# An encoder's second feed-forward layer: the sums of weights of all four units made in DRAM by accumulating transfers

## The chip, the core and the metric

One core of a Trainium2 chip runs the whole program. The metric is the device time of one execution in microseconds, of which the kernel before has three: 2171.28 (median), 2171.19 and 2171.61.

The core has five instruction streams: PE (TensorE, with its weight loads shown apart as PEld), DVE (VectorE), ACT (ScalarE), POOL (GpSimd) and SP (SyncE). Here SP does nothing but issue transfers, POOL issues the accumulating ones.

## The reference

Two layers over 256 positions of width 2048, in float32. Layer 0 has a mixer of pooling and attention, layer 1 one of matrix memory (mLSTM); each is followed by a gated MLP with a convolution of width 3 over positions. Cut to what matters here:

```python
def conv_ffn(x, w_up, conv_w, conv_b, w_down):
    u = x @ w_up
    up = jnp.pad(u, ((0, 0), (1, 1), (0, 0)))
    c = conv_w.astype(u.dtype)
    u = c[0] * up[:, :-2] + c[1] * up[:, 1:-1] + c[2] * up[:, 2:] + conv_b.astype(u.dtype)
    gate, val = jnp.split(u, 2, axis=-1)
    return (jax.nn.silu(gate) * val) @ w_down

def reference(...):
    for layer in range(DEPTH):
        ...
        x = x + mixed
        x = x + conv_ffn(rms_norm(x, norm_ffn[layer]), w_up[layer], conv_w[layer], conv_b[layer], w_down[layer])
    return x
```

`w_up` has 2048 x 11264 weights in each layer, `w_down` 5632 x 2048.

## The kernel before

**The stream of weights.** All weights pass through the class `Stream` in one order, in entries of up to 128 x 1024 values (512 KB). For each entry SP issues the load into a raw buffer `w`; ScalarE casts it to the high part of `hl` (line 164) and VectorE subtracts that from the raw values to get the low part (line 165). Three matmuls (high by high, high by low, low by high) then stand for one float32 matmul; all of them are recorded at line 285. Within a feed-forward layer up to 7 entries are loaded ahead and 3 split ahead; there are 7 raw buffers and 5 split ones, and a load waits until its raw buffer is free.

**The units.** An up-projection of one feature block is sixteen k-tiles (`up`, tile name `up`). Half of the blocks in the chunks 2 to 5 of a layer go another way, four blocks at a time: `quads` multiplies two by two blocks with seven products in place of eight (a Winograd form), on sums of activations (`sx`) and sums of weights; its tile is `p`. Such four blocks are a *unit*. A layer has four, in the chunks 2, 3, 4 and 5; the text calls them units 2, 3, 4 and 5 by their chunk. A unit takes 24 entries in a first part (16, called A and B below, in 8 pairs, and later 8 more, C) and four entries of plain weights (`b`). Between a unit's steps lie those of plain up-projections and of the down-projection (`dn`) of the chunk before.

**The table UNITS** has, for each unit, its chunk, its half, the first and last *slot* over which its steps are spread (a slot is one quarter of an `up` or two k-tiles of a `dn`, about one stream entry of plain weights), and a flag that says how its sums of weights come about:

- Flag 0: the raw weights are loaded as pieces of `in_q`, and VectorE makes the sums in the raw buffers, in `sums` (lines 144, 147, 149 and 150 of the profile): one add of 128 x 512 for an A entry, two for a B entry (the first of them reads the A entry's buffer too), one for a C entry. That is 32 adds a unit.
- Flag 1: the sums are made in DRAM ahead of time, in a tile `G` for each of the unit's eight pairs, and loaded like weights (kind "made" in `load`; an entry A or C is then two loads of 128 x 512, one from `G` and one from `in_q`).

**Making a pair in DRAM** is `make_step`, in four parts. Parts 0 and 1 each copy one half of the pair's rows from `in_q` to `G` on SP's queue (line 118), and then add other columns of `in_q` onto the copy by an accumulating transfer on POOL's queue (line 119). Parts 2 and 3 are accumulating transfers from `G` to `G` (line 123). The copies and the adds keep the program's order on their queues, so POOL waits at line 119 until the copy has landed. The list `places` says with which stream entry a pair's first part is issued and by how many entries the next ones follow.

Apart from PE, whose order is the program's, and the pinned instructions, a scheduler sets the order on each engine.

Of the kernel before, what the change touches and what calls it, by code (L numbers as in the profile page):

```python
# [64 lines left out]
class Stream:  # L65
# [56 lines left out]
            of = 0 if part == 2 else 1024  # L122
            pin(add.dma_start(G[:, at : at + 512], G[:, of : of + 512], accum_op=ALU.add))  # L123

    def prepare(self, kind, w):

        if kind[1] == 0:
            self.first = w
            return
        x, G = self.first, self.made_tile(kind[2])  # L130
        pin, add = self.tc.keep_in_program_order, self.nc.vector.tensor_add
        b11, b12, b22, b21 = (e[:, c : c + 512] for e in (x, w) for c in (0, 512))
        for to, other in ((b11, b12), (b12, b22), (b22, b11), (b21, b22)):
            pin(add(to, to, other))
        self.nc.gpsimd.dma_start(G[:, 0:1024], x)
        self.nc.gpsimd.dma_start(G[:, 1024:2048], w)

    def sums(self, i):
        if i in self.w and not self.w[i][4] and self.w[i][3] in ("sum", "chain", "left"):
            w, kind = self.w[i][0], self.w[i][3]  # L140
            l, r = w[:, 0:512], w[:, 512:1024]
            pin, add = self.tc.keep_in_program_order, self.nc.vector.tensor_add
            if kind == "sum":
                pin(add(r, r, l))
                self.sum = r
            if kind == "left":
                pin(add(l, l, r))
            if kind == "chain":
                pin(add(l, l, self.sum))
                pin(add(r, r, l))  # L150
            self.w[i][4] = True

    def split(self, then=None):
        i = self.n_split
        self.sums(i)
        w, n, width, kind = self.w.pop(i)[:4]
        if isinstance(kind, tuple):
            self.prepare(kind, w)
            self.n_split += 1
            self.sums(i + 1)  # L160
            return
        hl = self.home(i, False).tile([P, 2, CH * P], F32R, tag="hl", name=f"hl{i}")
        for c in range(0, width, n):
            (self.nc.vector.tensor_copy if i + c == 0 else self.nc.scalar.copy)(hl[:, 0, c : c + n], w[:, c : c + n])  # L164
            self.nc.vector.tensor_sub(hl[:, 1, c : c + n], w[:, c : c + n], hl[:, 0, c : c + n].bitcast(F32))  # L165
            then and then(c // n)
        self.hl[i] = hl
        self.n_split += 1
        self.sums(i + 1)

    def ahead(self, i, split=None):
        n = len(self.srcs)
        while self.n_load < min(n, i + self.la + 1):
            if self.n_load >= self.n_split + self.la - self.sa + 1:
                self.split()
            self.load()
        while self.n_split < min(n, i + (self.sa if split is None else split) + 1):
            self.split()

    def next(self):  # L180
        while self.is_prep(self.at):
            self.at += 1
        i = self.at
        self.ahead(i)
        self.at += 1
        return self.hl.pop(i)

    def is_prep(self, i):
        return isinstance(self.srcs[i], tuple) and isinstance(self.srcs[i][0], tuple)


class Weave:
# [6 lines left out]
    def add(self, gen, delay=0.0):  # L199
        self.q.append([self.t + delay, gen])  # L200
# [9 lines left out]
    def _run(self, e):  # L210

        try:
            d = next(e[1])
        except StopIteration:
            self.q.remove(e)
            return True
        e[0] = self.t + (d or 0.0)
        return d is not None
# [19 lines left out]
def trunk(ctx: ExitStack, tc: tile.TileContext, gx, xT, xn, call, catt, cml, weights, make, out):  # L238
# [239 lines left out]
    def attention_layer(norm, nxt):  # L478
        with ExitStack() as es:
# [11 lines left out]
            def block(ps, ti, dst, name):  # L491
# [33 lines left out]
                if name == "k":  # L525
                    yield from wv.wait(lambda: norm.blocks == NB)
                    fin = norm.finish()
                    yield next(fin)
                    rq = scales()
                    yield 4.0  # L530
                    for t in range(2):
                        r4 = rot[:, t, :].rearrange("p (h d) -> p h d", h=4)
                        v.tensor_mul(r4, r4, rq[:, 4 * t : 4 * t + 4].unsqueeze(2).to_broadcast([P, 4, P]))
                    yield 3.0
# [420 lines left out]
    def ffn_layer(layer, norm, nxt):  # L955
        with ExitStack() as es:
# [212 lines left out]
            for step in _ffn_plan(layer):  # L1169
                kind, c = step[:2]  # L1170
                key = step[:3]
                if key not in run:
                    f0 = sum(FCH[:c])
                    run[key] = (up(f0 + step[2], g_of(c), step[2]) if kind == "n" else
                                down(c, gts[c], step[2]) if kind == "d" else
                                quads([f0 + 4 * step[2] + j for j in range(4)], c, 4 * step[2], f"{layer}_{c}{step[2]}"))
                next(run[key], None)
# [64 lines left out]
def _down_chunks(w):  # L1242
# [7 lines left out]

UNITS = (
    ((2, 1, 18, 57, 1), (3, 1, 64, 90, 1), (4, 1, 97, 141, 0), (5, 1, 148, 174, 1)),
    ((2, 1, 18, 57, 1), (3, 1, 64, 90, 1), (4, 1, 97, 141, 0), (5, 1, 148, 174, 1)),
)


# [68 lines left out]
def _pairs(layer, four):  # L1325
    return [(f"{layer}{c}{h}_{p}", four[u, p]) for u, (c, h, _, _, made) in enumerate(UNITS[layer]) if made
            for p in range(KT // 2)]


def _with_prep(seq, pairs, first, gap):  # L1330

    out = []
    for i, e in enumerate(seq):
        n, r = divmod(i - first, gap)
        if r == 0 and 0 <= n < len(pairs):
            key, q = pairs[n]
            out += [(("prep", 0, key), q[:, 0:1024]), (("prep", 1, key), q[:, 1024:2048])]
        out.append(e)
    return out


def _make_steps(make, pairs, places):
# [113 lines left out]
```

## Time and profile before

| what | us |
|---|---|
| median of 3 runs | 2171.28 |
| the profiled execution's own time | 2171.85 |
| its span, first to last instruction | 2170.1 |
| second layer's feed-forward, first `up` to the end | 1449.8 to 2170.1 |
| its units 2, 3, 4, 5, first to last `p` | 1503.9 to 1644.3, 1671.3 to 1778.0, 1802.1 to 1959.3, 1986.2 to 2092.9 |
| first layer's units 2, 3, 4, 5 | 310.2 to 450.7, 477.6 to 584.3, 608.5 to 762.1, 788.9 to 895.6 |

The page gives each engine's busy time and its share of the span, the chain of work that ended last, and groups of like instructions. TensorE's clock was granted in full throughout. A row of a group reads: line, engine, operation, output and inputs, shape, count, then busy time in us, mean in ns, and the engine's idle time before them with what ended it. A row by stage gives, for each engine, busy us and the number of instructions in brackets, and at its end the granted clock, the DMA engines' share and the GB/s moved. A row of transfers gives the KB of one and the median of us from issue to landing. Matmuls are pipelined: the duration that is shown for one (0.39 us for 512 columns) is longer than the distance from one to the next.

### The profile page before, as it was taken

The page shows a single profiled execution, that of the slowest core. Times are in us where ns is not written, and L with a number is a line of the kernel's source. Part 1 is how long each engine was busy: PE and PEld are TensorE (multiplying, and loading weights), DVE is VectorE, ACT ScalarE, POOL GpSimd, SP SyncE. Part 2 cuts the span into 40 slices and gives each one's busy share as a digit, 9 for nine tenths or more (in the row PEclk, how much of TensorE's full clock was granted, in tenths as well). Part 3 has the DMA queues.
Part 4 walks back from the last instruction along what each step waited for, and adds up shares of the span by engine and source line. Part 5 has one row for each costly group of instructions (what it writes and reads, how often), then busy time and mean ns, then how long its engine had stood idle before and what let it go on. Part 6 is the DMA issues. An engine that isn't in the chain of part 4 may idle for free.

```text
span 2170.1 us, 30692 instructions
## 1 busy us (share of the span) xinstructions
PE 2162.6 (100%) x11040; PEld 1838.7 (85%) x11040; DVE 1679.4 (77%) x2350; ACT 1285.1 (59%) x1808; POOL 185.5 (9%) x232
## 2 busy tenths in 40 slices
PE   9999999999999999999999999999999999999999
PEld 7888888888888888889888888888888888788887
DVE  7686698787798787866767676769878778878785
ACT  7665565666665566655555454556566665557663
POOL 1121111110101000001111010110000000000000
PEclk9999999999999999999999999999999999999999
DMA  8878889999989978879788887888998997776873
GB/s 325 250 221 254 260 266 341 343 295 313 322 273 306 302 221 255 262 212 254 216 257 228 237 242 224 265 231 250 290 284 268 305 309 241 257 233 223 253 235 125
DMA packets 170268, 566.76 MB, mean 261 GB/s; under 512 B 20762, under 2 KB 23106, under 8 KB 168578
## 3 DMA queue, kind: packets, MB, share of 16 engines
q1 hardware_dynamic: 145376, 510.44, 68.3%
q0 software_dynamic: 21664, 50.61, 15.2%
q10 hardware_dynamic: 3074, 3.75, 0.8%
q8 instruction: 86, 1.41, 0.3%
q14 instruction: 68, 0.56, 0.1%
HBM read 562.57 MB, written 102.80 MB: 307 GB/s over the span
## 4 chain that ended last, share of the span: by engine, by line
PE 98%; DVE 1%; issue 0%; ACT 0%; DMA 0%; ACTq 0%; DVEq 0%
PE up L285 28%; PE dn L285 21%; PE p L285 14%; PE op L285 8%; PE mv L285 4%; PE mq L285 4%; PE mk L285 4%; PE mo L285 4%; PE qproj L285 3%; PE pool L285 1%; PE kproj L285 1%; PE vproj L285 1%; PE tr L1098 1%; PE av L285 1%; PE qk L285 1%; PE end L285 1%
## 5 line engine op out<-in xcount | busy, mean ns | idle before, releaser
L165 DVE TENSOR_TENSOR hl<-w,hl 128x1024 fp32r<-128x1024 f32 (+1 forms) x868 | 1049.8, 1218 | 344.9 <-ACT hl L164 336.7
L164 ACT CAST hl<-w 128x1024 fp32r<-128x1024 f32 (+1 forms) x867 | 902.9, 1049 | 645.7 <-PE up L285 163.4
L285 PE MATMUL up<-xx,hl 128*128 128x512 f32 (+1 forms) x3584 | 650.3, 337 | 0.0
L285 PEld LDWEIGHTS up<-xx,hl 128*128 128x128 f32 x3584 | 566.2, 188 | 88.4
L285 PE MATMUL dn<-hl,g 128*128 128x512 f32 x2064 | 491.8, 391 | 0.0
L285 PEld LDWEIGHTS dn<-hl,g 128*128 128x128 f32 x2064 | 384.9, 188 | 78.4
L285 PE MATMUL p<-hl,sx 128*128 128x512 f32 x768 | 204.5, 390 | 1.5 <-DVE hl L165 0.8
L119 POOL DMA_DIRECT2D G<-in_q x96 | 77.0, 802 | 1177.3 <-DMA G<-in_q 1165.7
L285 PEld LDWEIGHTS p<-hl,sx 128*128 128x128 f32 x768 | 139.2, 188 | 27.6 <-ACT hl L164 1.1
L285 PE MATMUL p<-hl,xx 128*128 128x512 f32 x576 | 156.4, 391 | 0.8 <-DVE hl L165 0.8
L285 PEld LDWEIGHTS p<-hl,xx 128*128 128x128 f32 x576 | 104.2, 188 | 20.7 <-DVE hl L165 1.7
L123 POOL DMA_DIRECT2D G<-G x96 | 89.2, 929 | 258.6 <-DMA G<-in_q 180.8
L285 PE MATMUL mk<-xx,hl 128*128 128x512 f32 (+1 forms) x512 | 92.2, 338 | 0.0
L285 PE MATMUL mq<-xx,hl 128*128 128x512 f32 (+1 forms) x512 | 92.2, 338 | 0.0
L285 PE MATMUL mv<-hl,xx 128*128 128x512 f32 (+2 forms) x480 | 91.8, 350 | 0.0
L285 PE MATMUL op<-hl,cat 128*128 128x512 f32 x384 | 91.6, 394 | 0.0
L285 PE MATMUL mo<-hl,xx 128*128 128x512 f32 x384 | 90.6, 392 | 0.0
L285 PE MATMUL op<-hl,mcat 128*128 128x512 f32 x384 | 89.5, 392 | 0.0
L285 PEld LDWEIGHTS mq<-xx,hl 128*128 128x128 f32 x512 | 79.4, 188 | 11.5
L285 PEld LDWEIGHTS mk<-xx,hl 128*128 128x128 f32 x512 | 79.2, 188 | 11.3
L285 PEld LDWEIGHTS mv<-hl,xx 128*128 128x128 f32 x480 | 78.3, 189 | 11.2
L285 PEld LDWEIGHTS op<-hl,mcat 128*128 128x128 f32 x384 | 71.5, 188 | 14.6
(243 smaller groups left out, 1831.7 us busy)
## 6 DMA issues: line engine op xcount, KB each, us to landing
w<-in_up SPq DMA_DIRECT2D x224, 512.0 KB, 5.3
w<-in_dn SPq DMA_DIRECT2D x176, 512.0 KB, 5.2
w<-in_m_in SPq DMA_DIRECT2D x124, 512.0 KB, 4.8
G<-in_q SPq DMA_DIRECT2D x96, 512.0 KB, 6.3
G<-in_q POOLq DMA_DIRECT2D x96, 256.0 KB, 6.5
G<-G POOLq DMA_DIRECT2D x96, 256.0 KB, 7.5
w<-in_q SPq DMA_DIRECT2D x96, 256.0 KB, 5.2
w<-G SPq DMA_DIRECT2D x96, 256.0 KB, 4.9
```

The lines of the kernel that those rows point to most:

```text
L119: pin(add.dma_start(G[r, 0:1024], src[r, 512:1536], accum_op=ALU.add))
L123: pin(add.dma_start(G[:, at : at + 512], G[:, of : of + 512], accum_op=ALU.add))
L164: (self.nc.vector.tensor_copy if i + c == 0 else self.nc.scalar.copy)(hl[:, 0, c : c + n], w[:, c : c + n])
L165: self.nc.vector.tensor_sub(hl[:, 1, c : c + n], w[:, c : c + n], hl[:, 0, c : c + n].bitcast(F32))
L285: pe.matmul(out_, lhsT, rhs, start=start, stop=stop, skip_group_check=True)
L1098: pe.transpose(tr[:, j, t * P : t * P + P], src[:, c : c + P], ident)
```

## The change

The second layer's unit 4 gets flag 1, so that all four of that layer's units have their sums made in DRAM. The slots of its units 3, 4 and 5 are laid out anew, and the second list of `places` has 32 pairs in place of 24. These pairs begin 200 entries ahead of the layer in place of 182, the first sixteen 12 entries apart in place of 13; the others follow 13 apart, with 6 entries between the parts, in place of 20 and 10. The first layer keeps its table and its places. What else is taken out (`prepare`, `is_prep`, `_with_prep`) is not reached in the kernel before: no entry of kind "prep" is ever made.

```diff
     def split(self, then=None):
         i = self.n_split
         self.sums(i)
-        w, n, width, kind = self.w.pop(i)[:4]
-        if isinstance(kind, tuple):
-            self.prepare(kind, w)
-            self.n_split += 1
-            self.sums(i + 1)
-            return
+        w, n, width = self.w.pop(i)[:3]
...
     def next(self):
-        while self.is_prep(self.at):
-            self.at += 1
         i = self.at
...
 UNITS = (
     ((2, 1, 18, 57, 1), (3, 1, 64, 90, 1), (4, 1, 97, 141, 0), (5, 1, 148, 174, 1)),
-    ((2, 1, 18, 57, 1), (3, 1, 64, 90, 1), (4, 1, 97, 141, 0), (5, 1, 148, 174, 1)),
+    ((2, 1, 18, 57, 1), (3, 1, 64, 95, 1), (4, 1, 102, 134, 1), (5, 1, 141, 174, 1)),
 )
...
-    places.append([(at - 182 + 13 * k, 6) for k in range(16)] + [(at + 26 + 20 * k, 10) for k in range(8)])
+    places.append([(at - 200 + 12 * k, 6) for k in range(16)] + [(at - 8 + 13 * k, 6) for k in range(16)])
```

Counted by entries of the second layer (0 is its first, 312 in all), the parts of the last eight pairs, those of unit 5, were issued from 26 to 196 and loaded from 233 on, the last at 258. Now they are issued from 96 to 205 and loaded from 226 on, one of them every 4 entries, the last at 255; those of unit 4 from -8 to 101, loaded from 159 on.

How the order moves is shown at three places. The first is VectorE in unit 4 of the second layer, a stretch of its first half. Before:

```order
L144 TENSOR_TENSOR w_16246<-w_16246 128x512
L976 SCALAR_TENSOR_TENSOR y_21_16286<-tb_up_21_16282,cst,y_21_16286 128x255 x2
L978 SCALAR_TENSOR_TENSOR y_21_16286<-tb_up_21_16282,cst,y_21_16286 128x255
L165 TENSOR_TENSOR hl_16361<-w_16297,hl_16361 128x1024
L978 SCALAR_TENSOR_TENSOR y_21_16286<-tb_up_21_16282,cst,y_21_16286 128x255
L149 TENSOR_TENSOR w_16309<-w_16309,w_16246 128x512
L165 TENSOR_TENSOR hl_16333<-w_16246,hl_16333 128x1024
L165 TENSOR_TENSOR hl_16350<-w_16259,hl_16350 128x1024
L982 TENSOR_TENSOR y_21_16286<-y_21_16286 128x256
L150 TENSOR_TENSOR w_16309<-w_16309 128x512
```

And now (line 165 has become 147, 982 and 984 are 959 and 961, and 459 is 436):

```order
L436 TENSOR_TENSOR x<-x,dn_2_1_16294 128x512
L959 TENSOR_TENSOR y_25_16331<-y_25_16331 128x256
L436 TENSOR_TENSOR x<-x,dn_2_1_16294 128x512
L147 TENSOR_TENSOR hl_16417<-w_16348,hl_16417 128x1024
L147 TENSOR_TENSOR hl_16438<-w_16365,hl_16438 128x1024
L961 TENSOR_TENSOR g_3_15871<-y_25_16331,g_3_15871 128x256
L147 TENSOR_TENSOR hl_16450<-w_16379,hl_16450 128x1024
L147 TENSOR_TENSOR hl_16471<-w_16401,hl_16471 128x1024
```

The adds onto `w` are gone; each raw chunk has one instruction on VectorE, its subtraction.

The second place is SP's queue at the start of unit 4's loads. Before:

```order
L100 DMA w_16038<-in_up 128x1024
L100 DMA w_16073<-in_q 128x1024
L118 DMA G_6_15848<-in_q 16x8192
L100 DMA w_16093<-in_up 128x1024
L100 DMA w_16129<-in_q 128x1024
L100 DMA w_16149<-in_dn 128x1024
```

And now:

```order
L100 DMA w_16116<-in_dn 128x1024
L93 DMA w_16136<-in_q 128x512
L93 DMA w_16136<-G_0_12743 128x512
L100 DMA w_16176<-in_dn 128x1024
L93 DMA w_16216<-G_0_12743 128x1024
L118 DMA G_5_16218<-in_q 16x8192
L100 DMA w_16240<-in_up 128x1024
```

The unit's entries are now loaded from `G`, an A entry in two pieces, and copies for unit 5 still go between them. In all SP has 32 more rows, POOL 32 more and VectorE 32 fewer.

The third place is POOL's queue in the matrix-memory mixer, at its first two heads, where POOL computes a reciprocal root for each (`ry_h`, line 292, now 269). Before:

```order
L119 DMA G_3_9230<-in_q 64x1024
L292 TENSOR_TENSOR ry_h_9519<-rv_h_9517,mhalf 128x2
L123 DMA G_3_9230<-G_3_9230 128x512
L119 DMA G_4_9611<-in_q 64x1024
L123 DMA G_3_9230<-G_3_9230 128x512
L292 TENSOR_TENSOR ry_h_9763<-rv_h_9761,mhalf 128x2
```

And now:

```order
L119 DMA G_5_9307<-in_q 64x1024
L269 TENSOR_TENSOR ry_h_9533<-rv_h_9531,mhalf 128x2
L123 DMA G_5_9307<-G_5_9307 128x512
L119 DMA G_6_9686<-in_q 64x1024
L269 TENSOR_TENSOR ry_h_9776<-rv_h_9774,mhalf 128x2
L123 DMA G_5_9307<-G_5_9307 128x512
```

The roots stand between the same kinds of transfers, of pairs two further on.

More of the change, by code (lines that the diff above doesn't have):

```diff
@@ L123, in make_step @@
             pin(add.dma_start(G[:, at : at + 512], G[:, of : of + 512], accum_op=ALU.add))
-    def prepare(self, kind, w):
-        if kind[1] == 0:
-            self.first = w
-            return
[L130 to L136, printed above, removed]
     def sums(self, i):
@@ L155, in split @@
         self.sums(i)
-        w, n, width, kind = self.w.pop(i)[:4]
-        if isinstance(kind, tuple):
-            self.prepare(kind, w)
-            self.n_split += 1
-            self.sums(i + 1)
-            return
+        w, n, width = self.w.pop(i)[:3]
         hl = self.home(i, False).tile([P, 2, CH * P], F32R, tag="hl", name=f"hl{i}")
@@ L186, in next @@
         return self.hl.pop(i)
-    def is_prep(self, i):
-        return isinstance(self.srcs[i], tuple) and isinstance(self.srcs[i][0], tuple)
 class Weave:
@@ L1327, in _pairs @@
             for p in range(KT // 2)]
[L1330 to L1339, printed above, removed]
 def _make_steps(make, pairs, places):
```

## The prediction

> **What bounds the kernel now.** I read the page first, its busy times and its chain.
>
> ```profile
> span 2170.1 us, 30692 instructions
> ...
> PE 2162.6 (100%) x11040; PEld 1838.7 (85%) x11040; DVE 1679.4 (77%) x2350; ACT 1285.1 (59%) x1808; POOL 185.5 (9%) x232
> ...
> PE 98%; DVE 1%; issue 0%; ACT 0%; DMA 0%; ACTq 0%; DVEq 0%
> ```
>
> TensorE carries 98% of the chain that ends last. The change leaves the number of matmuls and their operands' sizes as they are, so it can win only where TensorE starves now, and can lose only where it starves TensorE anew. The question is where TensorE starves. For that I read the busy times by stage, a stage being the time from the first to the last matmul of one unit (the tile p): two units of the first layer, then units 3 and 4 of the second.
>
> ```profile
> core 0: us, PE busy (x) PEld busy (x) DVE busy (x) ACT busy (x) POOL busy (x), PEclk, DMA share, GB/s
> 310.20:450.70 140.50, 140.50 (x730) 120.02 (x729) 112.83 (x144) 87.69 (x111) 21.05 (x26) 1.00 1.02 336
> 608.50:762.10 153.60, 153.60 (x762) 129.98 (x761) 129.48 (x163) 85.15 (x104) 14.37 (x18) 1.00 0.94 297
> 1671.30:1778.00 106.70, 106.70 (x522) 90.00 (x521) 81.96 (x94) 64.00 (x73) 8.14 (x10) 1.00 0.95 303
> 1802.10:1959.30 157.20, 154.87 (x761) 129.79 (x761) 129.43 (x163) 85.10 (x104) 4.07 (x5) 1.00 0.77 248
> ```
>
> ```profile
> L285 PE MATMUL p<-hl,xx x72: 388/390/396, 608.5 to 762.1; 128*128 128x512 f32 x72
> ...
> L285 PE MATMUL p<-hl,xx x72: 388/390/504, 1802.1 to 1959.3; 128*128 128x512 f32 x72
> ```
>
> The second and fourth stage are unit 4 of the first and of the second layer. Both have the same plan, both have their sums made by VectorE, and they have the same numbers of instructions on every compute engine but POOL to within one. The first takes 153.6 us with TensorE never idle. The second takes 157.2 us. So 3.6 us are lost in the second layer's unit 4, in the very unit that the change rewrites. The timeline of TensorE shows two of the places:
>
> ```profile
> 1854.91 0.39 PE L285 MATMUL p<-hl,xx 128*128 128x512 f32 x1
> 1855.86 0.74 PE L285 MATMUL p<-hl,xx 128*128 128x512 f32 x2 [0.56 <-DVE hl L165]
> 1856.44 0.86 PE L285 MATMUL p<-hl,sx 128*128 128x512 f32 x3
> 1857.14 0.39 PE L285 MATMUL up<-xx,hl 128*128 128x512 f32 x1
> ...
> 1879.19 2.88 PE L285 MATMUL dn<-hl,g 128*128 128x512 f32 x12
> 1882.79 0.49 PE L285 MATMUL p<-hl,sx 128*128 128x512 f32 x1 [0.73 <-ACT hl L164]
> 1884.06 0.73 PE L285 MATMUL p<-hl,sx 128*128 128x512 f32 x2 [0.77 <-DVE hl L165]
> 1884.63 0.85 PE L285 MATMUL p<-hl,xx 128*128 128x512 f32 x3
> ```
>
> Three such matmuls without a wait take from 1856.44 to 1857.14, 0.70 us, 0.23 each. The three from 1854.91 to 1856.44 took 1.53, so 0.83 is lost there, and by the same count about 2.0 is lost between 1879.19 and 1884.63 (fifteen matmuls at 0.23 would take 3.4; they took 5.44). Each time TensorE waits for a split chunk (hl). The chain of waits says why the chunk is late:
>
> ```profile
> 1844.33 0.61 DVE w L149
> ...
> 1844.96 6.72 DMA w<-in_up
> ...
> 1851.76 1.06 ACT hl L164
> ...
> 1853.98 0.69 DVE w L149
> 1854.67 1.14 DVE hl L165
> ...
> 1855.86 1.45 PE p L285 x5
> ```
>
> The add of line 149 reads the preceding "sum" chunk's buffer as well as its own, so that buffer is held until a later chunk has come and been added. Only then (1844.96) does the next load start, it lands 6.72 us later, and cast, another add and the subtraction follow in line before TensorE goes on.
>
> **The change part by part.** *Removed: 32 adds.*
>
> ```profile
> L165 DVE TENSOR_TENSOR hl<-w,hl 128x1024 fp32r<-128x1024 f32 x71 | 85.0, 1221 | 23.5 <-ACT hl L164 23.3
> ...
> L147 DVE TENSOR_TENSOR w<-w 128x512 f32<-128x512 f32 x8 | 5.5, 684 | 0.0
> L149 DVE TENSOR_TENSOR w<-w,w 128x512 f32<-128x512 f32 x7 | 4.8, 686 | 0.0
> L144 DVE TENSOR_TENSOR w<-w 128x512 f32<-128x512 f32 x7 | 4.8, 685 | 0.0
> L150 DVE TENSOR_TENSOR w<-w 128x512 f32<-128x512 f32 x7 | 4.8, 684 | 0.0
> ```
>
> Of these four groups the diff takes all 32 (three of them start just ahead of the stage): 32 x 0.685 = 21.9 us of VectorE. Nearly all of it lies beside matmuls and is worth nothing. What is worth something is the line that they form with the loads. With ready sums a chunk needs only its cast and its subtraction, and its buffer is free after the latter. The gain has two bounds. TensorE's idle time in the stage is 157.20 - 154.87 = 2.3 us, the low end; the same stage without stalls is 3.6 us shorter, the high end. I take 3.6, since it compares equal work, start to end. The Trainium skill, Perfetto Trace Analysis, section "Identifying the Most-Contended Engine", holds matmul busy time for a bad measure of TensorE, since matmuls are pipelined; the timeline agrees (idle of 0.56 is shown where 0.83 was lost). By the busy row the sum would be 2169.0, by the stages 2167.7.
>
> *Moved: the slots of units 3, 4 and 5.* Unit 3 goes from 26 slots to 31, unit 5 from 26 to 33, unit 4 from 44 to 32. A made unit in 26 slots runs without a stall now (1671.30 to 1778.00 above, TensorE busy throughout), so 31 to 33 slots cost nothing by that row; what hides it is the same splitting ahead. If it did not, a place like those above costs 0.8 to 2.0 us.
>
> *Added: eight more pairs made in DRAM, and all of the layer's pairs earlier and denser.* Each pair is two copies on SP's queue and four accumulating transfers on POOL's.
>
> ```profile
> q1 hardware_dynamic: 145376, 510.44, 68.3%
> q0 software_dynamic: 21664, 50.61, 15.2%
> ...
> G<-in_q SPq DMA_DIRECT2D x96, 512.0 KB, 6.3
> G<-in_q POOLq DMA_DIRECT2D x96, 256.0 KB, 6.5
> G<-G POOLq DMA_DIRECT2D x96, 256.0 KB, 7.5
> ...
> L123 POOL DMA_DIRECT2D G<-G x96 | 89.2, 929 | 258.6 <-DMA G<-in_q 180.8
> ...
> 1842.63 0.33 SPq L100 DMA_DIRECT2D w<-in_q  x1
> ```
>
> The 48 pairs of now take 15.2% of 2170.1 us on q0, 6.9 us of all sixteen DMA engines for each pair, and 96 copies of 0.524 MB at q1's 2.9 us per MB, 3.0 us for each pair: 9.9 us a pair. Eight more are 79 us, 3.7% of the span, all beside matmuls. POOL gets 32 more issues of at most 0.93 us, 30 us on an engine that is busy 9%. SP gets 32 more rows (16 copies, and 16 loads that now come in two pieces), at 0.33 us some 11 us; SP does nothing but issue. Unit 4's loads keep their bytes.
>
> What decides is the rate. The second feed-forward layer starts at 1449.8:
>
> ```profile
> 1449.77 3.47 PE up L285 x20
> ...
> 350.00:450.00 100.00, 100.00 (x521) 85.47 (x520) 78.50 (x99) 61.38 (x79) 15.36 (x19) 1.00 1.03 347
> ...
> w<-in_up SPq DMA_DIRECT2D x21, 512.0 KB, 9.7
> ...
> POOL ry_h L292 <- DVE rv_h L290: 125.3, 8, 22.3
> ```
>
> Its 312 stream entries take 2170.1 - 1449.8 = 720 us, 2.31 each. A pair every 20 entries is one in 46 us; every 13 entries, one in 30. The DMA share rises by 9.9/30 - 9.9/46 = 0.115: from 0.95 in unit 3's stage to about 1.06, and in unit 4's from 0.77 to about the same. (The share counts overlapping packets, so it can pass 1.) Between 350 and 450 us the kernel already runs at 1.03, with 19 accumulating transfers; a load then takes 9.7 us to land (the in_up row is of that window), and TensorE is busy for all of it. Loads run 7 entries ahead, 16 us. So I take nothing for the traffic; cover gone, the price is that of the rival below. The last pair is complete at entry 205, 50 entries (115 us) ahead of its load at 255.
>
> POOL also computes a reciprocal root for each of eight heads and for the norms. POOL waited for VectorE at all eight heads (125.3 us together), so no root stood behind a transfer. In the new order each still stands behind an accumulating transfer whose copy was issued shortly before; if one did arrive behind it, it would wait up to that copy's 6.3 us, and TensorE by what the head's delay leaves of that. I take 0, bounds 0 and 6.3 per head.
>
> **Sum.** The profiled execution took 2171.85 us, 0.57 above the median of 2171.28. 2171.85 - 3.6 = 2168.25; against the median, 2167.7 us, or 0.17% less. A difference of 0.2% is 4.3 us here, about what a measurement can tell from no change: below 2166.9 is faster, above 2175.6 slower.
>
> **The rivals.** *The loss stays (same).* Unit 4's stalls go, but its stage gets denser in chunks (44 slots to 32) and the order that the scheduler gives VectorE and ScalarE in units 3 to 5 is new. One stage of eight stalls now, so a reordered one may. Against it: all made stages run clean. One such stage costs 3.6, time 2171.3.
>
> *The DMA engines become the bound (slower).* If they sustain no more than the 1.02 of the stage at 310.20, the 1.06 to 1.07 that I expect from 1671 to about 1925 stretches 250 us by 4 to 5%: 10 to 13 us, time 2178 to 2181. It decides from a share above 1.04. For it: the loads' 9.7 us at 1.03. Against it: no stall there. The Trainium skill, DMA: Bandwidth & Descriptors, section "Specifications", gives about 358 GB/s as a core's limit to its memory. Unit 3's stage moves 303 GB/s and writes some 46 more in DRAM; the change makes that about 397, 11% over the limit, and the time some 2195. The trace disagrees: from 350 to 450 us 347 GB/s were moved and some 100 written on top, with TensorE busy throughout.
>
> *More is won (faster).* It would need 4.4 us; the stage offers 3.6, and elsewhere TensorE has no idle time that the change touches. 2166.5.
>
> **How the numbers follow.** Forecast 0.74; loss stays 0.14; DMA bound 0.08; more won 0.04. Hence faster 0.04, same 0.88, slower 0.08. The forecast's own range is 2167.0 to 2169.0 (its two bounds, and half a microsecond below). For 8 in 10 I reach up to the first rival: 2166.9 to 2171.3.
>
> **What would show it.** Right: no idle of TensorE in unit 4's stage, no line of the adds at 144 to 150 in the second layer, the end 3.6 us earlier with all stages before 1640 as now; a DMA share of 1.0 to 1.07 from 1550 to 1900 and loads landing in 7 to 10 us. Wrong: waits of p, up or dn for hl in units 3 to 5 with a load as the releaser (the DMA rival), or with ScalarE or VectorE (the first); heads' roots waiting behind POOL's transfers between 1040 and 1360.

## The result and the profile after

| kernel | median us | runs | lowest to highest |
|---|---|---|---|
| before | 2171.57 | 20 | 2171.00 to 2173.05 |
| the change | 2168.24 | 20 | 2168.09 to 2168.47 |

The ratio is 0.9984, with a 95% interval of 0.9978 to 0.9991. The medians differ by 3.3 us, the fastest executions by 2.9. The profiled execution took 2168.35 us (before 2171.85), with a span of 2166.6 us (before 2170.1), 3.5 us less by either. The page after shows the chain of waits as TensorE's alone, and the DMA queues with what the eight added pairs put on them:

```profile
span 2166.6 us, 30790 instructions
...
PE 2161.4 (100%) x11040; PEld 1838.1 (85%) x11040; DVE 1660.8 (77%) x2318; ACT 1286.0 (59%) x1808; POOL 211.6 (10%) x264
...
q1 hardware_dynamic: 148192, 518.83, 68.6%
q0 software_dynamic: 25248, 59.00, 17.4%
...
PE 100%; DVE 0%; issue 0%
```

VectorE has 32 instructions and 18.6 us fewer (1679.4 to 1660.8), POOL 32 more. What stands in the second layer is seen by stage. The rows are units 3, 4 and 5 of the changed kernel, each from its first matmul of tile p to its last:

```profile
1671.40:1792.00 120.60, 120.60 (x591) 101.73 (x590) 91.08 (x107) 71.36 (x83) 13.72 (x17) 1.00 1.00 320
1816.00:1936.60 120.60, 120.60 (x593) 101.82 (x593) 89.82 (x103) 70.82 (x82) 8.90 (x11) 1.00 0.92 290
1963.40:2086.70 123.30, 123.30 (x605) 104.06 (x604) 91.94 (x105) 72.42 (x86) 0.00 (x0) 1.00 0.76 243
```

TensorE is busy for the whole of each. These stages hold other numbers of plain steps than before (32 slots of them in unit 4 where there were 44), so their lengths are not compared with those of before; the waits are. The next rows are TensorE's list of waits: what waited, for what, the us in total, how often and the longest. First comes the kernel before in unit 4's stage, then the change over its whole span:

```profile
PE p L285 <- DVE hl L165: 1.6, 3, 0.8
PE p L285 <- ACT hl L164: 0.7, 1, 0.7
```

```profile
PE wps L286 <- DVE pad L655: 1.2, 1, 1.2
```

The four waits for split chunks are gone and no other has come; the 1.2 us are the program's start.

### The profile page after: what moved, and what is told of

It is laid out like the page before. It is cut to its first block, busy times and chain, and to the rows that moved or that the text cites. A ratio compares the mean times of both kernels' runs of the same rounds, so it can differ in the third digit from the quotient of the medians.

```text
span 2166.6 us, 30790 instructions
## 1 busy us (share of the span) xinstructions
PE 2161.4 (100%) x11040; PEld 1838.1 (85%) x11040; DVE 1660.8 (77%) x2318; ACT 1286.0 (59%) x1808; POOL 211.6 (10%) x264
## 3 DMA queue, kind: packets, MB, share of 16 engines
q0 software_dynamic: 25248, 59.00, 17.4%
## 4 chain that ended last, share of the span: by engine, by line
PE 100%; DVE 0%; issue 0%
PE up L262 29%; PE dn L262 22%; PE p L262 14%; PE op L262 8%; PE mv L262 4%; PE mq L262 4%; PE mk L262 4%; PE mo L262 4%; PE qproj L262 3%; PE kproj L262 1%; PE pool L262 1%; PE vproj L262 1%; PE tr L1075 1%; PE av L262 1%; PE qk L262 1%; PE end L262 1%
## 5 line engine op out<-in xcount | busy, mean ns | idle before, releaser
L119 POOL DMA_DIRECT2D G<-in_q x112 | 90.5, 808 | 1111.7 <-DMA G<-in_q 1098.9
L123 POOL DMA_DIRECT2D G<-G x112 | 102.1, 912 | 327.3 <-DMA G<-in_q 226.0
```

Of the source, the lines that this page charges most:

```text
L119: pin(add.dma_start(G[r, 0:1024], src[r, 512:1536], accum_op=ALU.add))
```

## The experiments

Each kernel ran beside runs of the kernel before on the same chip; ratios are against those. Times in us.

### The flag alone

The changed kernel, with the slots of before:

```diff
-    ((2, 1, 18, 57, 1), (3, 1, 64, 95, 1), (4, 1, 102, 134, 1), (5, 1, 141, 174, 1)),
+    ((2, 1, 18, 57, 1), (3, 1, 64, 90, 1), (4, 1, 97, 141, 1), (5, 1, 148, 174, 1)),
```

> Unit 4 of the second layer gets its sums from DRAM and the 32 pairs of the change are made at the change's places, but the slots of units 3, 4 and 5 stay as before (64 to 90, 97 to 141, 148 to 174). Theory (the loss came from the adds of unit 4 and goes with them): 3.3 to 3.6 us less than before, about 2168.2; unit 4's stage 153.6 us instead of 157.2, no wait of TensorE in it. Rival (the new slots bring the gain): no more than 1 us less than before. Rival (earlier and denser pairs cost something that the new slots hide): over 2169.5.

Measured: 2168.35, ratio 0.9985 (0.9976 to 0.9994). In this kernel unit 4's slots are those of before, so that its stage can be compared as it stands:

```profile
1802.30:1955.90 153.60, 153.60 (x762) 129.91 (x761) 112.21 (x132) 86.44 (x102) 9.54 (x12) 1.00 0.88 277
```

The stage took 157.2 us before and takes 153.6 now, with TensorE never idle. That is the 3.6 us of the prediction's comparison, with 17 us less work on VectorE. The whole gain is the flag's.

### The slots alone

The kernel before with the new slots and unit 4's sums still on VectorE:

```diff
-    ((2, 1, 18, 57, 1), (3, 1, 64, 90, 1), (4, 1, 97, 141, 0), (5, 1, 148, 174, 1)),
+    ((2, 1, 18, 57, 1), (3, 1, 64, 95, 1), (4, 1, 102, 134, 0), (5, 1, 141, 174, 1)),
```

> Only the slots of units 3, 4 and 5 of the second layer are those of the change; unit 4 keeps VectorE's sums and the 24 pairs their old places. Theory (the adds are the cause): the stalls of unit 4 do not go; its 32 adds now lie in 32 slots instead of 44, so they get worse, 1 to 8 us more than before (2172 to 2179). Rival (the slots bring the gain): 2 to 3.5 us less, about 2168.5.

Measured: 2175.42, ratio 1.0019 (1.0011 to 1.0028), 3.9 us slower. The profile is of the slowest of its eleven executions, 2178.18. By its list of waits TensorE stands still for 4.6 us in this stage, and the stage's row shows a granted clock (third number from the end) of 0.96:

```profile
PE p L285 <- DVE hl L165: 3.5, 2, 1.7
PE p L285 <- ACT hl L164: 1.1, 1, 1.1
...
1815.90:1946.40 130.50, 125.88 (x592) 105.18 (x592) 107.41 (x133) 70.70 (x85) 4.07 (x5) 0.96 0.78 245
```

The changed kernel's stage, with the same slots, takes 120.6 us, 9.9 less. So about half of that execution's loss is waiting, and the rest about what the clock takes: 0.04 x 130.5 = 5.2 us, an estimate. The tighter slots suit made sums; with VectorE's sums they cost. They bring none of the gain.

### The places alone

The kernel before, its 24 pairs made where the change makes its first 24, so that no accumulating transfer runs during unit 4:

```diff
-    places.append([(at - 182 + 13 * k, 6) for k in range(16)] + [(at + 26 + 20 * k, 10) for k in range(8)])
+    places.append([(at - 200 + 12 * k, 6) for k in range(16)] + [(at - 8 + 13 * k, 6) for k in range(8)])
```

> Only the places of the 24 pairs are moved, to those of the change's first 24, so that unit 5's pairs are complete before unit 4's stage begins and no accumulating transfer runs in it; sums and slots as before. Theory (adds): stalls remain, within 1.5 us of before. Rival (transfers for unit 5 in unit 4's stage made its loads late): 2 to 3.5 us less, about 2168.5.

Measured: 2171.20, ratio 0.9999 (0.9990 to 1.0008). In its profile three of the four waits stay, 1.7 us in all, though POOL does nothing in the stage; the one at 1855 us is missing. Transfers beside unit 4 were not the cause of the loss.

### No adds at all

The kernel before without the 32 adds of the second layer's unit 4:

```diff
             if kind == "sum":
-                pin(add(r, r, l))
+                self.skip or pin(add(r, r, l))
                 self.sum = r
...
```

and so for the three others, with `skip` set in the second layer.

> The kernel before with the 32 adds of the second layer's unit 4 left out and nothing put in their place (no sums in DRAM either, same loads, slots and places), so that part of the computation is missing. Theory (adds): TensorE's stalls in unit 4 go, 3.3 to 3.6 us less than before, about 2168.0; and the difference to the changed kernel, under 0.5 us, is all that the traffic of eight more pairs costs. Rival (late loads or the order of the queues, whatever the adds): within 1.5 us of before.

Measured: 2168.33, ratio 0.9984 (0.9975 to 0.9993). So the adds are the cause, and the kernel without them, which also has no pair of unit 4 to make, is not faster than the changed one (2168.24) or than the flag alone, which has its slots (2168.35): the eight pairs cost nothing.

### Is it the held buffer, or VectorE's time?

The prediction named the A entry's buffer, which the B entry's first add holds. Two kernels part the two. In the first the adds keep their time, but that add reads its own buffer:

```diff
-                pin(add(l, l, self.sum))
+                pin(add(l, l, r if self.layer else self.sum))
```

> The kernel before, except that in the second layer's unit 4 the first of a B entry's two adds reads that entry's own buffer in place of the A entry's, so the A entry's buffer is no longer held for it (the sums are then other ones). VectorE's 32 adds keep their time. Theory of the prediction (a held buffer makes the next load late): the stalls go, about 2168.2. Rival (the adds' 0.68 us each on VectorE, in line ahead of subtractions that TensorE needs): within 1 us of before, about 2171.

Measured: 2171.12, ratio 0.9997 (0.9988 to 1.0006). In the second only the add that holds the buffer is left in the second layer, over 8 columns instead of 512 (the first layer's branch keeps all adds):

```diff
-            if kind == "sum":
-                pin(add(r, r, l))
+            if self.layer == 0:
...
+            elif kind == "sum":
                 self.sum = r
...
+            elif kind == "chain":
+                pin(add(l[:, 0:8], l[:, 0:8], self.sum[:, 0:8]))
```

> The kernel before, except that of the 32 adds in the second layer's unit 4 only the eight that read the A entry's buffer are left, and these add 8 columns instead of 512; the sums are left out. So the buffer is held as before and VectorE's time for the adds is nearly gone. Theory of the prediction (held buffer): stalls stay, 2170.5 to 2171.5. Rival (VectorE's time): about 2168.3, as with no adds at all.

Measured: 2168.30, ratio 0.9985 (0.9976 to 0.9993). The rival holds in both: it is VectorE's time for the adds. The timeline of TensorE in the kernel without the hold shows which place goes all the same and which stays:

```profile
1855.03 0.97 PE L285 MATMUL p<-hl,xx 128*128 128x512 f32 x3
1855.84 0.86 PE L285 MATMUL p<-hl,sx 128*128 128x512 f32 x3
...
1882.19 0.51 PE L285 MATMUL p<-hl,sx 128*128 128x512 f32 x1 [0.73 <-ACT hl L164]
1883.45 0.73 PE L285 MATMUL p<-hl,sx 128*128 128x512 f32 x2 [0.75 <-DVE hl L165]
1884.02 0.85 PE L285 MATMUL p<-hl,xx 128*128 128x512 f32 x3
```

The wait at 1855, from which the prediction read the held buffer, is gone here; the larger one at 1882 is as before. In this one profile the stage took 156.5 us in place of 157.2, so at most 0.7 of the 3.6 us went with the hold, and the runs' interval does not tell it from nothing. The wait at 1855 is also missing in the profile of the places alone, where the hold stays and POOL's transfers are gone from the stage, so the hold alone does not make it. The fastest executions of the kernel before (2171.05 beside this one) are no slower than those without the hold (2171.05 to 2171.40); whether the wait comes in every execution of the kernel before is not shown.

At the larger place the chain of waits of the kernel before does not run through an add. It runs through ScalarE, where three activations of `c` stand between the casts, and then through the subtraction:

```profile
1878.07 0.68 ACT hl L164
...
1879.03 0.38 ACT c L1064
...
1879.61 0.68 ACT c L1065
1880.29 0.93 ACT hl L164
1881.22 0.59 ACT c L1066
1881.81 0.94 ACT hl L164
...
1882.77 1.24 DVE hl L165
```

The kernel without adds has the same three activations there and no wait. What the adds change is how far ahead the casts come. ScalarE's list of waits in the stage of before shows its casts waiting for adds, 28.5 us together; without the adds no cast waits for VectorE, and nearly all their waits end with a matmul. The rows of before:

```profile
ACT hl L164 <- DVE w L147: 13.3, 7, 2.1
ACT hl L164 <- DVE w L150: 10.1, 5, 3.1
ACT hl L164 <- DVE w L144: 5.1, 3, 2.4
```

In the first layer's stage the same rows come to 32.7 us, and TensorE never waits. So these waits alone do not decide; the time of the adds is shown as the cause, the step by which it becomes a stall at 1882 is not.

### Where the adds stand in the queue

The same 32 adds cost nothing in the first layer. In these two kernels all adds stay, but the program asks for a chunk's adds at its own split instead of one split earlier, once in the second layer and once in the first:

```diff
         self.hl[i] = hl
         self.n_split += 1
-        self.sums(i + 1)
+        self.layer or self.sums(i + 1)
```

> The kernel before, except that in the second layer's unit 4 the program asks for each chunk's adds at that chunk's own split and no longer one split earlier, so that they stand later in VectorE's queue; all 32 stay. Theory a (an add that stands ahead of a subtraction which TensorE needs sooner makes that one late): the stalls go or shrink, 2168.2 to 2169.7. Theory b (the sheer 21.9 us of VectorE in this stage): stalls stay, within 1 us of before, about 2171.3. Theory c (adds placed late delay their own chunk): more stalls, over 2172.5.

Measured: 2189.78, ratio 1.0078 (1.0065 to 1.0092).

> The kernel before, with the adds of the first layer's unit 4 (not the second's) asked for at their own chunk's split. That stage has the same plan and the same 32 adds, and no stall as it stands. Theory (the order in which the adds stand in VectorE's queue decides how much they cost, in either layer): the first layer's stage goes from 153.6 us to 168 to 175, 15 to 20 us more than before, about 2189. Rival (something of the second layer alone makes its adds cost time): within 2 us of before.

Here `or` is `and`. Measured: 2192.52, ratio 1.0099 (1.0082 to 1.0116), 21 us more than before, and the first layer's stage took 171.3 us (610.0 to 781.3). The second layer's stage in the former:

```profile
1804.10:1977.60 173.50, 161.53 (x760) 133.13 (x761) 130.90 (x157) 85.53 (x101) 4.07 (x5) 0.97 0.71 228
```

That is 173.5 us against 157.2, with hardly more work on VectorE (130.9 against 129.4 us) and VectorE idle for a quarter of it. TensorE is idle for 12 us of it; the granted clock of 0.97 takes some 5 us more (0.03 x 173.5, an estimate). The chain of waits in this kernel shows the form of it:

```profile
1892.19 0.97 DVE hl L165
...
1893.32 0.69 DVE w L150
1894.01 3.42 DVE hl L165 x3
...
1897.47 1.77 PE p L285 x5
```

An add and two other subtractions stand in line on VectorE ahead of the subtraction that TensorE needs, the last of the three. So it is not VectorE's total that costs here but whose turn it is: an add ahead of a needed subtraction, or an add ahead of its own chunk's cast (8.2 of TensorE's 13.2 us of waits end with a cast). Theory c held, and the first layer's run shows the same there. Why the scheduler's order of before happens to cost 3.6 us in the second layer and nothing in the first was not taken further apart.

### How much room was left for the traffic

Three kernels make pairs of units 4 and 5 a second time in the same stretch, into tiles that nothing reads: four, eight or sixteen of them. The edit for four:

```diff
         _make_steps(make, pairs[l], places[l])
+    for k in range(0, 16, 4):
+        key, q = pairs[1][16 + k]
+        _make_steps(make, [("x" + key, q)], [(at - 2 + 13 * k, 6)])
```

> The changed kernel with unit 4's and unit 5's sixteen pairs of the second layer made twice in the same stretch, the second time into tiles that nothing reads: a pair every 15 us, and a DMA share that would be 1.0 + 0.33 = 1.3 between about 1430 and 1900 us if all went through. Theory (the change's traffic is free because there is room above a share of 1.0): no more than 2 us above the changed kernel, under 2170.2, at a share no higher than 1.3 in that stretch. Rival (the engines are at their limit near 1.04): 10 us or more above it, TensorE waiting for loads. POOL's transfers, some 24 us a pair when each waits for the one before, may fall behind too; then SP's loads of G wait for them and TensorE stops by tens of us.

Measured: 2268.78, ratio 1.0445 (1.0431 to 1.0460).

> The changed kernel with four of unit 4's and 5's pairs made a second time, into tiles that nothing reads, spread over the same stretch. Theory (the DMA engines' ceiling is a share of about 1.035, as in the runs with too many pairs, and the stretch from 1430 to 1910 us runs at about 0.97 in the changed kernel): there is room for 0.065 x 480 = 31 us of all engines, three to four pairs at 8.4 to 9.9 us; so four more cost 0 to 8 us over the changed kernel, 2168 to 2176. Rival (no room is left at all): 34 to 40 us over it, above 2202.

Measured: 2168.28, ratio 0.9984 (0.9975 to 0.9993).

> The changed kernel with eight pairs of units 4 and 5 made a second time, into tiles that nothing reads, in the same stretch. Theory (a ceiling of about 1.035 and room for 31 us): eight more pairs need 67 to 79 us, so 35 to 46 us over the changed kernel, 2203 to 2214, TensorE waiting for chunks throughout units 3 to 5. Rival (the loss begins only beyond a pair in 20 us, which the first layer sustains): under 5 us over it, below 2173.

Measured: 2184.30, ratio 1.0057 (1.0044 to 1.0070). Against the changed kernel sixteen, four and eight more pairs are +100.5, 0 and +16 us. The stretch from 1430 to 1910 us by stage, with its DMA share as the last number but one: of the kernel before, of the change, and of the kernels with four and with eight more pairs.

```profile
1430.00:1910.00 480.00, 477.67 (x2437) 405.25 (x2437) 397.23 (x525) 293.71 (x385) 34.14 (x42) 1.00 0.87 270
```

```profile
1430.00:1910.00 480.00, 480.00 (x2453) 408.31 (x2453) 385.12 (x502) 299.02 (x388) 51.01 (x63) 1.00 0.95 296
```

```profile
1430.00:1910.00 480.00, 480.00 (x2454) 408.37 (x2453) 385.04 (x502) 298.90 (x388) 63.04 (x78) 1.00 0.99 312
```

```profile
1430.00:1910.00 480.00, 469.79 (x2377) 396.03 (x2376) 371.36 (x485) 287.24 (x375) 75.15 (x93) 0.99 1.02 318
```

The share does not go past 1.02 over this stretch, and past 1.04 in no slice of 50 us with eight or sixteen more pairs. There the engines are full, and it is loads that come late: by ScalarE's lists of waits its casts wait for loads to land for 2.6 us in the changed kernel, 52 us with four more pairs, 121 with eight and 226 with sixteen. The expectation of 1.3 for sixteen was wrong, that of 35 to 46 us for eight was more than twice too high, and the change itself lies at least four and fewer than eight pairs below the edge.

The other way to the edge is the first layer. The changed kernel with that layer's unit 4 made in DRAM too:

```diff
-    ((2, 1, 18, 57, 1), (3, 1, 64, 90, 1), (4, 1, 97, 141, 0), (5, 1, 148, 174, 1)),
+    ((2, 1, 18, 57, 1), (3, 1, 64, 90, 1), (4, 1, 97, 141, 1), (5, 1, 148, 174, 1)),
...
-    places = [[(24 + 19 * k // 2, 5) for k in range(16)] + [(len(att) + 110 + 14 * k, 7) for k in range(8)]]
+    places = [[(24 + 9 * k, 5) for k in range(32)]]
```

> The changed kernel with the first layer's unit 4 made in DRAM as well (its slots as before; the first layer's 32 pairs begin 9 entries apart). Theory (the gain is the stalls and nothing else; the first layer has none): 2168.2, within 0.5 us of the changed kernel, though VectorE loses 32 more adds. Rival (the DMA engines are near their limit, at a share of 1.03 there before): a pair in 21 us instead of 22 and eight more of them bring waits of TensorE for loads, 2 to 10 us more, 2170 to 2178.

Measured: 2191.39, ratio 1.0093 (1.0078 to 1.0109), 23 us above the change. The rival holds, and costs more than its 2 to 10 us. The stretch from 400 to 600 us in slices:

```profile
400.00:450.00 50.00, 47.31 (x240) 39.11 (x240) 32.69 (x41) 24.92 (x31) 6.57 (x8) 1.00 1.02 304
450.00:500.00 50.00, 46.03 (x230) 38.57 (x229) 44.78 (x69) 34.60 (x52) 8.20 (x10) 0.97 1.03 332
500.00:550.00 50.00, 50.00 (x241) 42.03 (x240) 36.04 (x41) 29.92 (x37) 8.18 (x10) 1.00 1.03 333
550.00:600.00 50.00, 47.11 (x227) 38.58 (x226) 31.51 (x35) 23.20 (x27) 6.56 (x8) 1.00 1.03 328
```

TensorE loses up to 4 us of 50 at a share of at most 1.03. The share was 1.02 from 310 to 450 us before, with TensorE never idle. ScalarE's casts wait 145 us for loads in this kernel, 9 in the kernel before. The first layer was nearly full already, and had no stall to win back.

## Why the prediction was right, and where it was not

**Where TensorE starves.** Right. The two equal stages of the prediction, 153.6 and 157.2 us, gave the size of the gain, and the flag alone turned the one into the other. Between the bounds of 2.3 (idle time as shown) and 3.6, the 3.3 us of the medians and the 3.5 of the profiled executions lie near the upper; the fastest executions differ by 2.9. The Trainium skill, Perfetto Trace Analysis, section "Identifying the Most-Contended Engine", holds matmul busy time for no good measure of how near TensorE is to its peak, because matmuls are pipelined. The trace agrees: the waits of before add up to 2.3 us, and 3.5 went.

**Why it starves.** The step that failed is the last of the part on what bounds the kernel: "so that buffer is held until a later chunk has come and been added". The chain of waits showed that sequence at one of the places, and it was taken for all of them. Without the hold the time stayed (2171.12); with the hold and without VectorE's time it fell (2168.30). What costs is VectorE's time for the adds, 0.68 us each; whether it reaches TensorE by a late subtraction or by a late cast was not shown for each place. The forecast did not depend on it, as the change takes both away.

**Moved slots at nothing.** Right (2168.35 without them, 2168.24 with).

**Added traffic at nothing.** Right in its price and wrong in its size and its margin. The share was to be 1.06 from 1671 us on; it was 1.00 in unit 3's stage and 0.92 in unit 4's. A pair takes less than reckoned. By the two pages q1 and q0 together went from 83.5% of 2170.1 us to 86.0% of 2166.6, which is 51 us for eight pairs, 6.4 us a pair and not 9.9. Most of the difference is q1's: its sixteen more copies were reckoned at 24 us, and its time rose by about 4. And unit 4's stage outlasts the making: from 1900 to 1950 us POOL issues nothing and the share is 0.77. The new slots have no part in this, as the flag alone, with the old ones, also shows 1.00 in unit 3's stage. Loads landed in some 7 us in unit 3's stage, as forecast, and in some 5 in unit 4's. The sentence that the share can pass 1 since packets overlap read as room what is the ceiling. What a share of 1.06 would have cost is seen with eight more pairs: at 6.4 us each they ask for 0.95 + 8 x 6.4 / 480 = 1.06, an estimate, and lost 16 us, where the rival said 10 to 13. Its bound, "a share above 1.04", is where the engines are full.

**The roots on POOL.** Right: POOL waits for VectorE before all eight heads' roots, 108.4 us together, as before 125.3.

```profile
POOL ry_h L269 <- DVE rv_h L267: 108.4, 8, 21.7
```

**The sum.** 2168.25 was forecast for the profiled execution and 2168.35 measured. Against the median it was 2167.7, and 2168.24 measured. The 0.5 us between lie in the kernel before: its executions vary by 2 us, the profiled one stood above the median of the first three, and the term of 3.6 was taken from it, while the fastest execution of before (2171.00) lies only 2.8 above the changed kernel's median. The changed kernel's twenty runs lie within 0.4 us.

**The rival of no change** (a new stall in the reordered units) did not come, and the one of a larger gain could not: with no adds and no pairs the time is 2168.33.

## What to carry to other kernels

Look for two stages of one plan within one trace: their difference in length is the price of a stall, and tells it better than idle time does. Before blaming a dependence that a chain of waits shows at one place, take it away alone and keep the engine's time; here it was the engine's time, and the same adds, asked for one split later, cost 18 to 21 us. Sums made by transfers are free only while the DMA engines have room. The sign that it runs out is the time that loads take to land, before TensorE waits: 5 to 7 us in units 3 and 4 of the changed kernel, 10 to 11 from 1700 to 1900 us with four more pairs (TensorE still never waiting there), 12 to 13 with eight.

## What the runs showed of the hardware that was not expected

**The DMA engines are full at a share of 1.03.** No slice of 50 us of an overloaded stretch shows more than 1.05. With eight more pairs the share from 1700 to 1900 us is 1.03 and a load takes 12 us to land, nearly the 16 us by which loads run ahead:

```profile
w<-in_dn SPq DMA_DIRECT2D x25, 512.0 KB, 12.0
w<-in_up SPq DMA_DIRECT2D x24, 512.0 KB, 12.7
```

An accumulating transfer is dear: 17.4% of 2166.6 us on q0 for 56 pairs, four transfers each, is 1.7 us of packet time of all sixteen engines for 0.26 MB, where q1's plain transfers take 2.9 us per MB, 0.75 us for as much.

**A short stall can cost TensorE half its clock for 3.4 us.** In one profile (the places alone) the granted clock, the third number from the end, falls behind the stall at 1882:

```profile
1879.00:1884.40 5.40, 3.90 (x16) 2.72 (x15) 4.86 (x7) 4.97 (x8) 0.00 (x0) 1.00 0.84 275
1884.50:1887.90 3.40, 3.40 (x10) 2.63 (x9) 2.84 (x5) 1.04 (x1) 0.00 (x0) 0.50 0.92 302
1888.00:1892.00 4.00, 4.00 (x23) 3.41 (x22) 2.85 (x4) 1.05 (x1) 0.00 (x0) 1.00 0.55 201
```

TensorE was idle for 1.5 us in all, and then ran ten matmuls at half speed; that execution took 2173.04 us where the median is 2171.20. The kernel before has the same stall, and its profile kept the full clock. The Trainium skill, TensorE: Matmul & The Clock Gate, section "Part 1: The HAM clock gate (the 'warmup' mystery)", tells of a free-running window of some 3.4 us and of half the clock after at least one idle window. The trace agrees on the 3.4 us and the half, but 1.5 us of idleness in two pieces were enough here.

For most runs the mean granted clock is on record to three decimals, and 3.4 us at half speed in 2171 us would show there as 0.999. Where the stalls are longer, the clock sorts the times: the slots alone took 2173.98 and 2174.05 us at 1.0, 2175.19 to 2175.42 at 0.999, 2176.94 to 2177.14 at 0.998 and 2178.18 at 0.997. It does not explain the spread of the kernel before: of its 76 runs beside the other kernels only the two slowest (2173.24 and 2173.45 us) show 0.999, and the others, up to 2172.99 us, show 1.0. A drop too short for three decimals, of at most 1.1 us of lost time, is not excluded there. What else moves these runs by up to 2 us is open; those of the change, without the stalls, lie within 0.4.
